# Two-layer retention and gated-linear-attention backbone: norms and slab splits taken off GpSimd

## Chip, cores, metric

One NeuronCore of a Trainium2 chip runs the whole program. The metric is device microseconds of one execution, the median of several runs. Before the change three runs took 1653.16, 1654.71 and 1655.32 us.

## What is computed

Two layers act on a stream of 512 latent tokens and a prefix of 256 context tokens, 1024 features each, in float32:

```python
for layer in range(DEPTH):                       # DEPTH = 2
    need_ctx = layer < DEPTH - 1
    sh1, sc1, g1, sh2, sc2, g2 = split(silu(c) @ ada_w[layer] + ada_b[layer])
    hx = modulate(rmsnorm(x, norm1_g[layer]), sh1, sc1)
    hc = modulate(rmsnorm(ctx, norm1_g[layer]), csh1, csc1)
    mx, mc = hybrid_mixer(hx, hc, ...)           # 4 retention heads, 4 GLA heads
    x = x + g1 * (mx @ w_out[layer])
    hx = modulate(rmsnorm(x, norm2_g[layer]), sh2, sc2)
    x = x + g2 * squared_relu_mlp(hx, w_mlp1[layer], w_mlp2[layer])
    if need_ctx:
        ...
return rmsnorm(x, final_g)
```

`modulate(h, shift, scale)` is `h * (1 + scale) + shift`. The mixer projects the normed tokens with `w_in` (3616 columns) into queries, keys, values, gates and the low-rank decay, runs both scans of each head over chunks, and normalises each head before the output projection. Layer 2 needs no context output.

## The kernel before

**Layout.** The activations stand transposed: eight tiles `x_0` to `x_7` of 128 features by 768 tokens, latents in columns 0 to 511 and context in 512 to 767. Every float32 product is made of three products of rounded parts, `hi*hi + hi*lo + lo*hi` (`mm3`, lines 433 to 436; `project`, lines 438 to 457). So each weight slab of 128x1024 and each activation is split into a rounded `hi` and a rest `lo`.

**Slabs.** A `Slab` is loaded by SP into one of four `raw` buffers; `split` (lines 241 to 245) writes `hi` with ScalarE (ACT) and `lo` with the slab's `engine`, VectorE (DVE) by default, GpSimd (POOL) for a few. Slabs 5 and 6 of layer 2's `w_in` go to GpSimd (lines 691, 692). `hi` and `lo` have six buffers each. `run` (lines 386 to 424) walks a plan of items; before an item it splits the slabs that the item needs and `item.ahead` more (4 unless the item says otherwise), and after an item with slabs up to four more than it needed.

**Norms.** `Norm.stat` (line 485) sums squares over features with a matmul by `ones_d` (tile `st_n`), and ACT makes the reciprocal root from it (tile `ssum_n`, lines 494 and 495). `Norm.apply` (lines 506 to 523) then turns each of the eight tiles into `hi` and `lo`. It has two forms. The usual one: DVE writes `xn = x*scale*rstd` (L519), ACT writes `hi` (L521), DVE writes `lo` (L523). The other one, for every third tile (`kk % 3 == 2`, tiles 2 and 5): GpSimd writes `x*rstd` (L512), ACT writes `hi` (L514) and the scaled value again (L515), DVE writes `lo` (L517). A chain runner (`Chains`) keeps three tiles under way and interleaves their steps with other work, one step at each tick.

**Layer 2's start.** While TensorE (PE) still works on the last MLP products of layer 1 for the context columns (tiles `pm`, whose sums DVE adds to `x` on L537), the norm of the latents runs. Then the item `firsts0` (function `together`) multiplies tile after tile with the first three slabs 0, 1 and 3 into three banks `ps_d`, `ps_gq`, `ps_gk`; after tile 5 it calls the norm of the context columns. `firsts1` does slabs 0 and 3 for the context, then the item `firsts` evacuates those banks, and the values `vg` follow with slabs 5 to 8 (block `vg0`, tiles `ps_vg`).

**Evacuating heads.** `dup_evac` (lines 720 to 735) copies a bank that holds two heads, 64 rows each, into one 128-row tile per head, the 64 rows twice (`d` is the half of the destination, `i` the head). In layer 1, for heads 0 and 1, half `d = 0` goes to ACT and half `d = 1` to DVE. All else is ACT's.

**Order.** In-layer stages stand in the table `SCHEDULE` (lines 107 to 132); each row's entries are run in order, in both layers. `g2qk` is the stage in which DVE multiplies the queries (L847) and keys (L848) of GLA head 2, the third head, by their decays; `g2S` makes their score products (tiles `psf`, `psb`, L869). `qa0` and `qb0` project the retention queries of heads 0 and 1 (`ps_qa`, `ps_qb`); DVE evacuates `ps_qa` with L950 and L951. `g0A` and its like make the decay (tile `pgl`, L814). `g1N` makes a head's norm (tile `hs`, L794).

PSUM has seven banks in rotation (`ps`): a new tile waits until the tile seven allocations back has been read.

Of the kernel before, what the change touches and what calls it, by code (L numbers as in the profile page):

```python
# [12 lines left out]
AF = mybir.ActivationFunctionType  # L13
ALU = mybir.AluOpType
# [100 lines left out]
vr2 g0D g1K tabs  # L115
gq1 g1D g0O g3A
gk1 g1O g0N g3B
qa0 g2qk g1N g3C
qb0 g2S g2K g3qk
ka0 g3S g3K g2D  # L120
kb0 g3D g2O
# [17 lines left out]
def build(ctx: ExitStack, tc, a):  # L139
    nc = tc.nc  # L140
# [14 lines left out]
    ch = Chains()  # L155

    def bank(name):
        return ps.tile([P, 512], F32, tag="ps", name=name)

    def work(name, dt=F32):  # L160
        return mp.tile([P, T], dt, tag="m", name=name)

    def temp(name):
        return tmp_pool.tile([P, LAT], F32, tag="t", name=name)

    def f32(ap):
        return ap.bitcast(F32)
# [275 lines left out]
    def project(pt, slab, c0, acts, t0, t1, ks=None, first=0, last=None):  # L443

        ks = range(len(acts)) if ks is None else ks
        last = len(acts) - 1 if last is None else last
        out = pt[:, 0 : t1 - t0]
        for k in ks:
            acts[k].ready(ch, t0, t1)
            xh, xl = acts[k].hi[:, t0:t1], acts[k].lo[:, t0:t1]  # L450
            w = slice(c0 + k * P, c0 + k * P + P)
            if isinstance(slab, RankSlab):
                nc.tensor.matmul(out, slab.hi[:, w], xh, start=k == first, stop=False)
                nc.tensor.matmul(out, slab.hi[:, w], xl, start=False, stop=k == last)
            else:
                mm3(out, slab.hi[:, w], slab.lo[:, w], xh, xl, k == first, k == last)
        ch.tick()


    class Norm:  # L460
# [42 lines left out]
                    op0=ALU.add, op1=ALU.mult,  # L503
                )

        def apply(self, kk, l, shift, v, t0, t1, pool=False):
            hh, hl = self.out[kk].hi[:, t0:t1], self.out[kk].lo[:, t0:t1]
            xn = temp(f"xn_{self.name}_{kk}_{t0}")[:, 0 : t1 - t0]
            x, rstd = xs[kk][:, t0:t1], self.ssum[:, t0:t1]
            scale, bias = self.s[:, v, kk : kk + 1], mod[l][:, v, shift + kk : shift + kk + 1]  # L510
            if pool:
                nc.gpsimd.tensor_mul(xn, x, rstd)  # L512
                yield
                nc.scalar.activation(hh, xn, AF.Identity, scale=scale, bias=bias)  # L514
                nc.scalar.activation(xn, xn, AF.Identity, scale=scale, bias=bias)  # L515
                yield
                nc.vector.tensor_sub(hl, xn, f32(hh))  # L517
            else:
                nc.vector.scalar_tensor_tensor(xn, x, scale, rstd, op0=ALU.mult, op1=ALU.mult)  # L519
                yield  # L520
                nc.scalar.activation(hh, xn, AF.Identity, bias=bias)  # L521
                yield
                nc.vector.scalar_tensor_tensor(hl, xn, bias, f32(hh), op0=ALU.add, op1=ALU.subtract)  # L523

        def apply_all(self, l, shift, v, t0, t1, ks=range(KK)):

            for kk in ks:
                if self.out[kk] is None:
                    self.out[kk] = Act(
                        work(f"hh_{self.name}_{kk}", F32R), work(f"hl_{self.name}_{kk}", F32R)  # L530
                    )
            for kk in ks:
                c = ch.queue(self.apply(kk, l, shift, v, t0, t1, kk % 3 == 2))
                self.out[kk].made.append((t0, t1, c))

    def residual(kk, pt, l, gate, v, t0, t1):
# [34 lines left out]
    def start_project(q, groups):  # L571
        for j in START:
            for t0, t1 in groups:
                if q == 0:
                    acc0[j, t0] = bank(f"ps0_{j}_{t0}")
                project(acc0[j, t0], sl0[j], 0, norm0.out, t0, t1, (2 * q, 2 * q + 1), 0, KK - 1)
# [23 lines left out]
    def quarter_step(q):  # L600
        quarter_chain[q] = quarter(q)
        start_project(q - 1, ALLG)

    def quarter_finish(q):
        quarter_end(q, quarter_chain[q])
        quarter_norm(q, ALLG)
        for _ in range(6):
            ch.tick()
# [3 lines left out]
    def load_late():  # L612
        for name, shape in (("delta", [P, P]), ("ramp", [P, 2, P]), ("cosT", [P, LAT]), ("sinT", [P, LAT])):
            late[name] = load_const(name, shape)
# [42 lines left out]
    def layer(l, norm):  # L657
# [8 lines left out]
        pre = f"L{l}."  # L666
        tabs = {}

        def start():
            raw = temp(f"upraw_{l}")  # L670
            nc.sync.dma_start(raw, a["upw"][l])
            upw = tabs["upw"] = tp.tile([P, NH, P], F32R, tag="upw", name=f"upw_{l}")
            raw = raw.rearrange("p (h m) -> p h m", h=NH)
            nc.scalar.copy(upw, raw)
            nc.vector.tensor_sub(upw[96:128], raw[96:128], f32(upw[96:128]))

            tabs["ret"] = tp.tile([P, NH, 3, P], F32, tag="rtab", name=f"rtab_{l}")
# [10 lines left out]
            nc.vector.tensor_scalar(rtab[:, h, 1:3], rtab[:, h, 1:3], RET_SCALE, None, op0=ALU.mult)  # L688

        sl = [(Slab if j else RankSlab)(w_in[j], f"wi{l}_{j}") for j in range(29)]  # L690
        for j in (5, 6) if l else ():
            sl[j].engine = nc.gpsimd

        def feat(j, name, groups, evac):
            def fn():
# [26 lines left out]
        def dup_evac(lst, hp2, nm, sc):  # L722
            def ev(p_, t0, t1):
                for i in range(2):
                    h = 2 * hp2 + i
                    if t0 == 0:
                        lst[h] = work(f"{nm}_{l}_{h}")
                    for d in range(2):
                        dst, src = lst[h][64 * d : 64 * d + 64, t0:t1], p_[64 * i : 64 * i + 64]
                        if d and l == 0 and hp2 == 0:  # L730
                            nc.vector.tensor_scalar(dst, src, sc, None, op0=ALU.mult)
                        else:
                            nc.scalar.mul(dst, src, sc)

            return ev
# [358 lines left out]
        if l == 0:  # L1094

            def head():
                start()
                load_late()
                for j, _, groups, ev in firsts:
                    for t0, t1 in groups:  # L1100
                        ev(acc0[j, t0][:, 0 : t1 - t0], t0, t1)

            plan = [
                Item(pre + "norm", start_norms, ahead=0),
                Item(pre + "q3", lambda: quarter_step(3), ahead=0),
                Item(pre + "q3n", lambda: quarter_finish(3), ahead=0),
                Item(pre + "q3p", lambda: start_project(3, ALLG), ahead=0),
                Item(pre + "head", head, ahead=4),
            ]
        else:  # L1110
            done = []

            def together(i):

                todo = [(j, bank(f"ps_{nm}_1_{groups[i][0]}"), *groups[i], ev)
                        for j, nm, groups, ev in firsts if i < len(groups)]
                for kk in range(KK):
                    for j, pt, t0, t1, _ in todo:
                        project(pt, sl[j], 0, act, t0, t1, [kk], 0, KK - 1)
                    if kk == 5 and i == 0:  # L1120
                        next_norm(norm, l, 1)
                done.extend(todo)

            def evacuate():
                while done:
                    _, pt, t0, t1, ev = done.pop(0)
                    ev(pt[:, 0 : t1 - t0], t0, t1)

            plan = [
                Item(pre + "start", start),  # L1130
                Item(pre + "firsts0", lambda: together(0), [sl[j] for j in (0, 1, 3)]),
                Item(pre + "firsts1", lambda: together(1), [sl[j] for j in (0, 3)]),
                Item(pre + "firsts", evacuate),
            ]
# [214 lines left out]
    for l in range(DEPTH):  # L1349
        items, norm = layer(l, norm)  # L1350
        plan += items
# [97 lines left out]
```

## Time and profile before

| | before |
|---|---|
| runs | 1653.16, 1654.71, 1655.32 us (median 1654.71) |
| the profiled execution | 1652.87 us, of which its span 1651.1 us |
| mean granted TensorE clock | 0.998 |
| PE busy | 1619.0 us, 98% of the span, 9306 matmuls |
| DVE, ACT, POOL busy | 945.2 us (57%), 629.5 us (38%), 191.2 us (12%) |
| DMA | 173.82 MB, mean 105 GB/s |

A matmul's busy time reaches past the start of the next, so a gap in PE is shorter than the time between the starts suggests. The times of a row are counted from the span's start. "x2" at the end of a row means two instructions merged, with the time of both; what stands in brackets is the idle time of the engine before it and what ended it.

### The profile page before, as it was taken

The page shows a single profiled execution, that of the slowest core. Times are in us where ns is not written, and L with a number is a line of the kernel's source. Part 1 is how long each engine was busy: PE and PEld are TensorE (multiplying, and loading weights), DVE is VectorE, ACT ScalarE, POOL GpSimd, SP SyncE. Part 2 cuts the span into 40 slices and gives each one's busy share as a digit, 9 for nine tenths or more (in the row PEclk, how much of TensorE's full clock was granted, in tenths as well). Part 3 has the DMA queues.
Part 4 walks back from the last instruction along what each step waited for, and adds up shares of the span by engine and source line. Part 5 has one row for each costly group of instructions (what it writes and reads, how often), then busy time and mean ns, then how long its engine had stood idle before and what let it go on. Part 6 is the DMA issues. An engine that isn't in the chain of part 4 may idle for free. (4 is left out here: it accounts for less than half of the span.)

```text
span 1651.1 us, 23033 instructions
## 1 busy us (share of the span) xinstructions
PE 1619.0 (98%) x9306; PEld 1386.0 (84%) x9306; DVE 945.2 (57%) x1494; ACT 629.5 (38%) x1085; POOL 191.2 (12%) x211
## 2 busy tenths in 40 slices
PE   6999999999999999999999999999999999999997
PEld 4778788888898888888888888888889988888887
DVE  5675664554755555555556476688466743343445
ACT  5635333562532222222212246363464623223232
POOL 2000022110111010110101121002111301010010
PEclk9999999999999999999999999999999999999999
DMA  9443333122323333333433222121124322323311
GB/s 327 147 142 129 127 115 116 39 101 78 103 90 128 115 128 112 118 102 115 128 115 128 90 81 79 52 76 52 52 67 139 116 92 99 100 92 102 102 64 52
DMA packets 57611, 173.82 MB, mean 105 GB/s; under 512 B 6208, under 2 KB 17792, under 8 KB 57504
## 3 DMA queue, kind: packets, MB, share of 16 engines
q1 hardware_dynamic: 55232, 164.85, 30.5%
q0 software_dynamic: 2272, 7.50, 1.3%
q8 instruction: 73, 1.20, 0.3%
q14 instruction: 34, 0.28, 0.1%
HBM read 168.13 MB, written 4.19 MB: 104 GB/s over the span
## 5 line engine op out<-in xcount | busy, mean ns | idle before, releaser
L440 PE MATMUL pm<-yl,hi_m 128*128 128x512 f32 (+1 forms) x808 | 279.7, 346 | 1.1 <-DVE yl L517 0.6
L439 PE MATMUL pm<-yh,hi_m 128*128 128x512 f32 (+1 forms) x808 | 279.8, 346 | 0.0
L439 PE MATMUL pm<-hidh,hi_m 128*128 128x512 f32 (+1 forms) x800 | 279.1, 349 | 0.0
L441 PE MATMUL pm<-yh,lo_m 128*128 128x512 f32 (+1 forms) x808 | 278.7, 345 | 0.0
L440 PE MATMUL pm<-hidl,hi_m 128*128 128x512 f32 (+1 forms) x800 | 278.4, 348 | 0.0
L441 PE MATMUL pm<-hidh,lo_m 128*128 128x512 f32 (+1 forms) x800 | 277.2, 347 | 0.0
L1220 ACT ACTIVATE relu<-pm 128x512 f32<-128x512 f32 (+1 forms) x101 | 51.3, 508 | 493.0 <-PE pm L441 493.0
L1224 DVE TENSOR_TENSOR hidl<-relu,hidh 128x512 fp32r<-128x512 f32 (+1 forms) x101 | 61.7, 613 | 290.0 <-POOL relu L1222 290.0
L537 DVE SCALAR_TENSOR_TENSOR x<-pm,mod,x 128x512 f32<-128x512 f32 (+1 forms) x200 | 117.6, 640 | 108.8 <-PE pm L441 108.8
L1222 POOL TENSOR_TENSOR relu<-relu 128x512 f32<-128x512 f32 (+1 forms) x101 | 90.6, 898 | 755.9 <-ACT hidh L1221 755.6
L440 PEld LDWEIGHTS pm<-yl,hi_m 128*128 128x128 f32 x808 | 153.1, 189 | 20.8 <-DVE yl L523 1.2
L439 PEld LDWEIGHTS pm<-yh,hi_m 128*128 128x128 f32 x808 | 153.0, 189 | 19.9 <-issue 1.2
L439 PEld LDWEIGHTS pm<-hidh,hi_m 128*128 128x128 f32 x800 | 151.4, 189 | 21.2 <-issue 1.1
L441 PEld LDWEIGHTS pm<-yh,lo_m 128*128 128x128 f32 x808 | 153.0, 189 | 18.7
L441 PEld LDWEIGHTS pm<-hidh,lo_m 128*128 128x128 f32 x800 | 151.1, 189 | 19.6
L440 PEld LDWEIGHTS pm<-hidl,hi_m 128*128 128x128 f32 x800 | 151.4, 189 | 19.0 <-issue 0.2
L245 DVE TENSOR_TENSOR lo_m<-raw_m,hi_m 128x1024 fp32r<-128x1024 f32 x126 | 153.9, 1222 | 10.1 <-ACT hi_m L244 10.1
L244 ACT CAST hi_m<-raw_m 128x1024 fp32r<-128x1024 f32 x128 | 129.8, 1040 | 52.1 <-DMA raw_m<-in_w_mlp 28.8
L345 DVE SCALAR_TENSOR_TENSOR adaacc<-adaw,cs,adaacc 128x1024 f32<-128x1024 f32 x84 | 103.9, 1278 | 0.0
L245 DVE TENSOR_TENSOR lo_wi<-raw_wi,hi_wi 128x1024 fp32r<-128x1024 f32 x54 | 66.4, 1247 | 28.1 <-ACT hi_wi L244 27.9
L439 PE MATMUL pwo<-yh,hi_wo 128*128 128x256 f32 (+1 forms) x224 | 70.9, 316 | 0.1
L440 PE MATMUL pwo<-yl,hi_wo 128*128 128x256 f32 (+1 forms) x224 | 70.3, 314 | 0.3 <-DVE yl L1068 0.3
(306 smaller groups left out, 2934.2 us busy)
## 6 DMA issues: line engine op xcount, KB each, us to landing
raw_m<-in_w_mlp SPq DMA_DIRECT2D x128, 512.0 KB, 3.5
adaw<-in_ada_w SPq DMA_DIRECT2D x80, 512.0 KB, 3.8
raw_wi<-in_w_in SPq DMA_DIRECT2D x58, 512.0 KB, 4.4
adaw<-in_ada_w SPq DMA_DIRECT2D x32, 256.0 KB, 6.0
raw_wo<-in_w_out SPq DMA_DIRECT2D x16, 512.0 KB, 3.5
x<-in_xT POOLq DMA_DIRECT2D x8, 384.0 KB, 8.0
x<-in_xT SPq DMA_DIRECT2D x8, 256.0 KB, 5.0
raw_wob<-in_w_out SPq DMA_DIRECT2D x4, 512.0 KB, 3.9
```

Of the source, the lines that this page charges most:

```text
L244: nc.scalar.copy(self.hi, self.raw)
L245: self.engine.tensor_sub(self.lo, self.raw, f32(self.hi))
L345: nc.vector.scalar_tensor_tensor(acc[:, v], w, c, acc[:, v], op0=ALU.mult, op1=ALU.add)
L439: nc.tensor.matmul(out, wh, xh, start=first, stop=False)
L440: nc.tensor.matmul(out, wh, xl, start=False, stop=False)
L441: nc.tensor.matmul(out, wl, xh, start=False, stop=last)
L537: nc.vector.scalar_tensor_tensor(xs[kk][:, t0:t1], pt[:, 0 : t1 - t0], mod[l][:, v, gate + kk : gate + kk + 1], xs[kk][:, t0:t1], op0=ALU. ...
L1220: nc.scalar.activation(r, pt[:, 0 : t1 - t0], AF.Relu)
L1222: nc.gpsimd.tensor_mul(r, r, r)
L1224: nc.vector.tensor_sub(a_.lo[:, t0:t1], r, f32(a_.hi[:, t0:t1]))
```

## The change

1. `Norm.apply` loses its GpSimd form. Tiles 2 and 5 of every norm take the usual form: for each of the norms' column groups (16 tile pieces in all) a GpSimd product (L512) and an ACT pass (L515) go, a DVE product (L519) comes.
2. Slabs 5 and 6 of layer 2's `w_in` get their `lo` from DVE.
3. Layer 2's items `start` and `firsts0` get `ahead=0`: no slabs beyond those needed are split before them.
4. In layer 1 the bank of heads 0 and 1 is evacuated with head 0's tile by ACT alone and head 1's by DVE alone.
5. `g2qk` moves ahead of `qa0` in the table.

```diff
-qa0 g2qk g1N g3C
+g2qk qa0 g1N g3C
...
-        def apply(self, kk, l, shift, v, t0, t1, pool=False):
+        def apply(self, kk, l, shift, v, t0, t1):
...
-            if pool:
-                nc.gpsimd.tensor_mul(xn, x, rstd)
-                yield
-                nc.scalar.activation(hh, xn, AF.Identity, scale=scale, bias=bias)
-                nc.scalar.activation(xn, xn, AF.Identity, scale=scale, bias=bias)
-                yield
-                nc.vector.tensor_sub(hl, xn, f32(hh))
-            else:
-                nc.vector.scalar_tensor_tensor(xn, x, scale, rstd, op0=ALU.mult, op1=ALU.mult)
-                yield
-                nc.scalar.activation(hh, xn, AF.Identity, bias=bias)
-                yield
-                nc.vector.scalar_tensor_tensor(hl, xn, bias, f32(hh), op0=ALU.add, op1=ALU.subtract)
+            nc.vector.scalar_tensor_tensor(xn, x, scale, rstd, op0=ALU.mult, op1=ALU.mult)
+            yield
+            nc.scalar.activation(hh, xn, AF.Identity, bias=bias)
+            yield
+            nc.vector.scalar_tensor_tensor(hl, xn, bias, f32(hh), op0=ALU.add, op1=ALU.subtract)
...
-                c = ch.queue(self.apply(kk, l, shift, v, t0, t1, kk % 3 == 2))
+                c = ch.queue(self.apply(kk, l, shift, v, t0, t1))
...
-        for j in (5, 6) if l else ():
-            sl[j].engine = nc.gpsimd
...
-                        if d and l == 0 and hp2 == 0:
+                        if i and l == 0 and hp2 == 0:
                             nc.vector.tensor_scalar(dst, src, sc, None, op0=ALU.mult)
                         else:
                             nc.scalar.mul(dst, src, sc)
...
-                Item(pre + "start", start),
-                Item(pre + "firsts0", lambda: together(0), [sl[j] for j in (0, 1, 3)]),
+                Item(pre + "start", start, ahead=0),
+                Item(pre + "firsts0", lambda: together(0), [sl[j] for j in (0, 1, 3)], ahead=0),
```

What this does to the order of instructions, at three places. First, DVE at the norm of the latents ahead of layer 2; `xn_n_1_K` and `hl_n_1_K` are tile K's product and rest, `x_2` the sum over the last MLP product. Before:

```order
L523 SCALAR_TENSOR_TENSOR hl_n_1_1_8394<-xn_n_1_1_0_8421,mod_150,hh_n_1_1_8393 128x512
L519 SCALAR_TENSOR_TENSOR xn_n_1_3_0_8442<-x_3_3369,mods_n_1_8384,ssum_n_1_8224 128x512
L517 TENSOR_TENSOR hl_n_1_2_8396<-xn_n_1_2_0_8434,hh_n_1_2_8395 128x512
L519 SCALAR_TENSOR_TENSOR xn_n_1_4_0_8449<-x_4_3371,mods_n_1_8384,ssum_n_1_8224 128x512
L537 SCALAR_TENSOR_TENSOR x_2_3367<-pm_0_7_2_512_8409,mod_149,x_2_3367 128x256
...
L523 SCALAR_TENSOR_TENSOR hl_n_1_3_8398<-xn_n_1_3_0_8442,mod_150,hh_n_1_3_8397 128x512
L523 SCALAR_TENSOR_TENSOR hl_n_1_4_8400<-xn_n_1_4_0_8449,mod_150,hh_n_1_4_8399 128x512
```

After:

```order
L511 SCALAR_TENSOR_TENSOR xn_n_1_2_0_8426<-x_2_3363,mods_n_1_8376,ssum_n_1_8216 128x512
L515 SCALAR_TENSOR_TENSOR hl_n_1_1_8386<-xn_n_1_1_0_8413,mod_150,hh_n_1_1_8385 128x512
L511 SCALAR_TENSOR_TENSOR xn_n_1_3_0_8433<-x_3_3365,mods_n_1_8376,ssum_n_1_8216 128x512
L515 SCALAR_TENSOR_TENSOR hl_n_1_2_8388<-xn_n_1_2_0_8426,mod_150,hh_n_1_2_8387 128x512
L511 SCALAR_TENSOR_TENSOR xn_n_1_4_0_8440<-x_4_3367,mods_n_1_8376,ssum_n_1_8216 128x512
L529 SCALAR_TENSOR_TENSOR x_2_3363<-pm_0_7_2_512_8401,mod_149,x_2_3363 128x256
...
L515 SCALAR_TENSOR_TENSOR hl_n_1_3_8390<-xn_n_1_3_0_8433,mod_150,hh_n_1_3_8389 128x512
L511 SCALAR_TENSOR_TENSOR xn_n_1_5_0_8452<-x_5_3369,mods_n_1_8376,ssum_n_1_8216 128x512
L245 TENSOR_TENSOR lo_wi_5_8457<-raw_wi_5_8370,hi_wi_5_8456 128x1024
L515 SCALAR_TENSOR_TENSOR hl_n_1_4_8392<-xn_n_1_4_0_8440,mod_150,hh_n_1_4_8391 128x512
```

DVE has two products of tiles 2 and 5 and one slab split more; the sum `x_2` has one more product ahead of it.

Second, ACT at the norm of the context columns in layer 2 (`hi_wi_J` are slabs, `hh_n` the norm's `hi` tiles). Before:

```order
L674 CAST upw_8551<-upraw_8549 128x512
L244 CAST hi_wi_6_8557<-raw_wi_6_8463 128x1024
L244 CAST hi_wi_7_8563<-raw_wi_7_8555 128x1024
L494 ACTIVATE ssum_n_1_8224<-st_n_1_512_8618,epst 128x256
L495 ACTIVATE ssum_n_1_8224<-ssum_n_1_8224 128x256
...
L521 ACTIVATE hh_n_1_7_8405<-xn_n_1_7_512_8651,mod_150 128x256
L244 CAST hi_wi_8_8716<-raw_wi_8_8561 128x1024
```

After:

```order
L666 CAST upw_8541<-upraw_8539 128x512
L494 ACTIVATE ssum_n_1_8216<-st_n_1_512_8596,epst 128x256
L495 ACTIVATE ssum_n_1_8216<-ssum_n_1_8216 128x256
...
L513 ACTIVATE hh_n_1_7_8397<-xn_n_1_7_512_8627,mod_150 128x256
L244 CAST hi_wi_6_8650<-raw_wi_6_8454 128x1024
L244 CAST hi_wi_7_8656<-raw_wi_7_8648 128x1024
L244 CAST hi_wi_8_8704<-raw_wi_8_8654 128x1024
```

Slabs 6 and 7 now stand behind the norm of the context instead of ahead of its root; on DVE the split of slab 7, which stood ahead of the first product of this norm, and that of slab 6 stand behind its last rest in the same way.

Third, DVE around `g2qk` in layer 2. Before:

```order
L833 TENSOR_TENSOR gt_3_9417<-gt_3_9417,gst_3_9513 128x768
L245 TENSOR_TENSOR lo_wi_17_9522<-raw_wi_17_9429,hi_wi_17_9521 128x1024
L950 TENSOR_TENSOR rq_0_0_9550<-ps_qa_0_0_9525,c_cosT 64x512
L951 TENSOR_TENSOR rq_0_0_9550<-ps_qa_0_0_9525,c_sinT 64x512
L950 TENSOR_TENSOR rq_0_1_9551<-ps_qa_0_0_9525,c_cosT 64x512
L951 TENSOR_TENSOR rq_0_1_9551<-ps_qa_0_0_9525,c_sinT 64x512
L847 TENSOR_TENSOR gq_2_9377<-gq_2_9377,gt_2_8827 128x512
L848 TENSOR_TENSOR gk_2_9460<-gk_2_9460,gl_2_8828 128x768
```

After:

```order
L823 TENSOR_TENSOR gt_3_9405<-gt_3_9405,gst_3_9501 128x768
L837 TENSOR_TENSOR gq_2_9365<-gq_2_9365,gt_2_8815 128x512
L838 TENSOR_TENSOR gk_2_9448<-gk_2_9448,gl_2_8816 128x768
L245 TENSOR_TENSOR lo_wi_17_9512<-raw_wi_17_9417,hi_wi_17_9511 128x1024
L940 TENSOR_TENSOR rq_0_0_9540<-ps_qa_0_0_9515,c_cosT 64x512
L941 TENSOR_TENSOR rq_0_0_9540<-ps_qa_0_0_9515,c_sinT 64x512
```

The two products stand ahead of a slab split and of the four operations that evacuate `ps_qa`. On PE the order is the same except for one place in layer 1, where the two `hs` products of `g1N` come ahead of the transposes `adat` (L268) instead of behind them. SP's queue keeps its order. POOL has 18 instructions less.

## Rows read from the trace of the kernel before

**Rows 1.** Waits of PE: who for whom, us in total, times, the longest.

```profile
PE st_n L492 <- DVE ssum_n L475: 1.8, 2, 1.3
PE adat L268 <- ACT adarow L263: 1.7, 3, 0.7
PE ps_d L453 <- ACT hh_n L521: 1.5, 1, 1.5
...
PE psf L869 <- DVE gk L848: 1.0, 1, 1.0
PE ps_gq L439 <- DVE x L537: 1.0, 1, 1.0
PE pm L440 <- DVE yl L517: 0.6, 2, 0.4
```

**Rows 2.** Timeline of PE, layer 1: start, length, engine, line, tiles, [idle before].

```profile
70.95 0.38 PE L814 MATMUL pgl<-dT,upw 128*128 128x256 f32 x1 [1.43 <-ACT vg L775]
71.63 0.50 PE L439 MATMUL ps_vg<-hi_wi,hh_n 128*128 128x512 f32 x1 [0.30 <-ACT vg L775]
```

**Rows 3.** Timeline of ACT, the first evacuations of layer 1.

```profile
60.59 0.59 ACT L733 ACTIVATE gq<-ps 64x512 f32<-64x512 f32 x1
...
67.84 0.38 ACT L733 ACTIVATE gk<-ps 64x256 f32<-64x256 f32 x1 [0.80 <-DVE gk L731]
...
70.13 1.45 ACT L775 COPY vg<-ps_vg 128x128 f32<-128x128 f32 x8
```

**Rows 4.** Timeline of ACT, the first evacuations of layer 2.

```profile
1003.70 2.40 ACT L733 ACTIVATE gq<-ps_gq 64x512 f32<-64x512 f32 x4
...
1008.81 1.55 ACT L733 ACTIVATE gk<-ps_gk 64x256 f32<-64x256 f32 x4
...
1012.42 0.78 ACT L775 COPY vg<-ps_vg 128x128 f32<-128x128 f32 x4
```

**Rows 5.** Timeline of DVE around `g2qk` in layer 2.

```profile
1103.93 1.22 DVE L245 TENSOR_TENSOR lo_wi<-raw_wi,hi_wi 128x1024 fp32r<-128x1024 f32 x1
...
1108.48 0.95 DVE L848 TENSOR_TENSOR gk<-gk,gl 128x768 f32<-128x768 f32 x1
```

**Rows 6.** Timeline of DVE, the norms ahead of layer 2.

```profile
971.10 2.45 DVE L519 SCALAR_TENSOR_TENSOR xn_n<-x,mods_n,ssum_n 128x512 f32<-128x512 f32 x2
...
975.90 1.56 DVE L517 TENSOR_TENSOR hl_n<-xn_n,hh_n 128x512 fp32r<-128x512 f32 x1
...
981.21 2.90 DVE L519 SCALAR_TENSOR_TENSOR xn_n<-x,mods_n,ssum_n 128x512 f32<-128x512 f32 x1
...
992.48 2.58 DVE L245 TENSOR_TENSOR lo_wi<-raw_wi,hi_wi 128x1024 fp32r<-128x1024 f32 x1 [1.18 <-ACT hi_wi L244]
994.98 1.80 DVE L519 SCALAR_TENSOR_TENSOR xn_n<-x,mods_n,ssum_n 128x256 f32<-128x256 f32 x2
```

**Rows 7.** Timeline of POOL in the same stretch.

```profile
981.00 2.56 POOL L245 TENSOR_TENSOR lo_wi<-raw_wi,hi_wi 128x1024 fp32r<-128x1024 f32 x1 [4.08 <-ACT hi_wi L244]
```

**Rows 8.** Timeline of DVE, the same operations while POOL is idle.

```profile
48.24 1.42 DVE L519 SCALAR_TENSOR_TENSOR xn_n<-x,mods_n,ssum_n 128x512 f32<-128x512 f32 x2
...
1275.21 0.47 DVE L519 SCALAR_TENSOR_TENSOR xn_n<-x,mods_n,ssum_n 128x256 f32<-128x256 f32 x1
1275.60 0.47 DVE L537 SCALAR_TENSOR_TENSOR x<-pwo,mod,x 128x256 f32<-128x256 f32 x1
```

**Rows 9.** Timeline of PE: the sum of the context norm of layer 2.

```profile
990.63 0.70 PE L492 MATMUL st_n<-ssum_n,ones_d 128*128 128x256 f32 x2 [1.33 <-DVE ssum_n L475]
```

**Rows 10.** Timeline of ACT: the root for the context norm of layer 2.

```profile
992.35 0.47 ACT L494 ACTIVATE ssum_n<-st_n,epst 128x256 f32<-128x256 f32 x1
```

**Rows 11.** Timeline of PE where `vg0` of layer 2 begins.

```profile
1003.65 0.40 PE L439 MATMUL ps_vg<-hi_wi,hh_n 128*128 128x512 f32 x1
```

**Rows 12.** PE in two windows: length, busy (instructions), granted clock, DMA share, GB/s.

```profile
997.90:1001.40 3.50, 3.50 (x18) 0.53 0.14 59
1001.40:1004.00 2.60, 2.60 (x22) 0.98 0.00 0
```

## Prediction

> **What bounds the kernel now.** I read the busy times first (the table above). PE is busy 98% of the span, so time can come only from the few places where PE stands still. The second view is the list of waits: whom PE waits for. Of the waits that bear on this change, a reader should see how short they are and that each names one engine [rows 1]: 1.5 us for ACT's `hi` of the context norm in layer 2, 1.3 us for the sum of squares ahead of it, 1.0 us for DVE's evacuation of the old MLP bank, 1.0 us for the keys of `g2qk`, 0.7 us for an ACT copy ahead of `adat`, 0.6 us for rests of layer 2's second norm. In layer 1, PE stands 1.43 and 0.30 us because ACT copies `vg` too late [rows 2]. The third view is the timeline around these places. It gives the causes, and one more loss: after the waits in layer 2's start, 18 matmuls take 3.50 us at a granted clock of 0.53 (the 1.2 GHz level), where 22 of the same size then take 2.60 us at 0.98 [rows 12]. At that pace 18 need 2.1 us, so 1.4 us are lost though PE counts as busy.
>
> **First evacuation, layer 1.** ACT and DVE write halves of the same tile, and they alternate: ACT's eight copies run from 60.59 to 68.22 us, each waiting for DVE's half [rows 3]. In layer 2 ACT makes such copies alone without a wait, at 0.60 us (four in 2.40) and 0.39 us (four in 1.55) [rows 4]. With a head per engine ACT needs 4 x 0.60 + 4 x 0.39 = 4.0 us instead of 7.6 and is through at 64.6, 3.6 us earlier. The copies of `vg` then begin at 66.5 instead of 70.13, and the first bank is free by 67.3; PE asks for it at 70.95 - 1.43 = 69.5. The second bank's product ends only just before that, and its four copies take 0.7 us (half of 1.45), so it is free at about 69.5 too. Both waits go: 1.7 us. Bounds 0.8 (the second copies slip) and 2.0.
>
> **`g2qk` moved.** Its keys end at 1108.48 + 0.95 = 1109.4; PE waited 1.0 us for them. What now stands behind them is a slab split of 1.22 us and four evacuations that fill the time until the two products begin [rows 5], so they end some 3.9 us earlier, near 1105.5. The wait goes: 1.0 us. The price is that `ps_qa` is evacuated 1.6 us later (the two products); its bank is next wanted after one projection and the score products, about a microsecond behind that. Bounds 0.2 and 1.0. In layer 1 the same move brings the `hs` products ahead of `adat`, into the 0.7 us in which PE waits for ACT's copy [rows 1]; their input was made before. 0.7 us, bounds 0 and 0.7.
>
> **Norm without GpSimd, layer 2's start.** This is the largest term.
> Ahead of layer 2 DVE has no idle time until the sum of squares is through, so its work there sets when PE may go on. With POOL idle, a product of 512 columns takes 0.71 us (two in 1.42), and operations of 256 columns follow each other every 0.39 us [rows 8]. Beside POOL's norm and slab work they take far longer [rows 6]: two products 2.45 us, one rest 1.56 us, one product 2.90 us, which ends half a microsecond after POOL's 2.56 us split [rows 7]. The excess is 1.03 + 0.85 + 2.19 = 4.1 us. Added are two products (2 x 0.71) and the split of slab 5 (1.22, as in [rows 5]): 2.6 us. The sum comes 1.4 us earlier, at 989.2. The evacuation for which PE waits 1.0 us at the start has +0.71 and -1.9 us ahead of it, so that wait goes, and PE, arriving 1.0 us earlier at the sum, still waits some 0.9 us there instead of 1.33 [rows 9].
> ACT's root could have begun at 990.63 + 0.70 = 991.3; it began at 992.35, behind slabs 6 and 7 [rows 10]. And DVE began the first product only at 994.98, behind slab 7's split of 2.58 us [rows 6]. Both stand behind the norm now: root at 989.9, first product at 990.9, 4.1 us earlier. Sixteen operations at 0.40 us and the first handover of 0.7 us end at 998.0. PE reaches the context columns near 993.5 and needs 40 x 0.118 = 4.7 us at full pace [rows 12], so it ends near 998.5; now `vg0` begins at 1003.65 [rows 11]. That is 5.1 us, of which the slow stretch is 1.4.
> What it costs: slabs 6, 7 and 8 are split after the norm. ACT's casts come from 997.2 on, DVE's splits end near 999.4, 1000.6 and 1001.8 at 1.22 us each. PE wants slab 6 about 1.6 us into `vg0`, at 1000.1, and another every 1.4 us. The margin is about half a microsecond. ACT's evacuations move up by only 3.1 us, so its copies of `vg` begin at 1009.3 instead of 1012.42 [rows 4], and PE waits about 0.3 us for the second bank. Net 4.8 us; bounds 1.0 (first rival) and 5.6.
> The Trainium skill speaks against this part: Perfetto Trace Analysis, section Optimizing Scalar/DVE Operations, says that offloading work to other engines, even GPSIMD, may make sense if DVE is saturated, which it is here (though it adds that between those two it might not help). By that rule, taking the work back would lengthen the stretch; by the rows it shortens it. The rule's outcome is the third rival below.
>
> **The other norms.** The second norm of layer 2 gains the waits for its rests, 0.6 us [rows 1], for the same reason; bounds -0.9 (two more products of 0.47 us [rows 8], nothing relieved) and 0.9. In the first norm of layer 1 and its second norm PE hardly waits for rests, so the two products more are hidden behind PE's work and paid for by POOL's silence: 0, bounds -0.5 and 0.5. ACT loses a pass per piece, which nobody waits for.
>
> **Sum.** 1.7 + 1.0 + 0.7 + 4.8 + 0.6 = 8.8 us. On the profiled execution of 1652.87 us that gives 1644.1. The median of the runs, 1654.71, is 1.8 us above that execution, so the forecast for the median is **1645.9 us**.
>
> **Rivals.**
> First, *the start of layer 2 stays held by what now follows the norm*. If a pair of product and rest costs 1.1 us instead of 0.8, the rests end 2.4 us later, slab 6 comes after PE wants it, and a pause there costs a slow stretch of 1.4 us again. The term falls to 1.0, the sum to 5.0: 1649.7. For it speaks the margin of half a microsecond; against it that the rests' pace is taken from rows.
> Second, *the waits only move to the next in line*. If ACT's evacuations keep their time in layer 2 (copies of `vg` at 1012.42), PE gets its bank 3.1 us later than walked and the term is 1.7; if in layer 1 DVE's half holds the bank and `ps_qa`'s bank is late, those give 0.8 and 0.2. With the 0.7 that is 3.4 or less: 1651.3 and above, within what a measurement of this kernel can tell from no change (0.2%, 3.3 us). Against it: ACT's string has nothing else ahead of it.
> Third, slower: *DVE is saturated and not relieved*. If its long operations ahead of layer 2 are not POOL's doing, the sum comes 2.6 us later instead of 1.4 earlier, the root at 994.9, and 16 operations at 0.90 us (half of 1.80 [rows 6]) end near 1010.0. `vg0` begins 6.4 us later than now, and the second norm loses 0.9. With 1.7, 1.0 and 0.7 gained that is 3.9 us slower: 1658.6. It decides once `vg0` begins later than about 1006.1, when the loss at both norms outweighs the 3.4 us. Against it: with POOL idle the same operations take 0.71 and 0.39 us.
>
> **Numbers.** Forecast 0.72, first rival 0.15, second 0.08, third 0.05. Faster by over 0.2%: forecast and first rival, 0.87; within 0.2%: 0.08; slower: 0.05. All upper bounds together are 10.7 us, 1644.0; the three runs differ by 2.2 us, so the range begins 1.5 us below that, at 1642.5. It goes to 1650.5, which takes in the first rival with half that scatter and leaves out the other two.
>
> **What would show it.** Right: no idle bracket at the sixth `pgl` in layer 1; ACT's eight copies there without gaps, done by 65 us; DVE's 512-column products ahead of layer 2 all near 0.74 us; `vg0` of layer 2 beginning about 5 us earlier relative to the last MLP product than now, with no window at half clock before it; no wait of `psf` for the keys. A wait of about 0.9 us for the sum of squares remains. Wrong: PE waiting for `lo` of slabs 6 to 8 in `vg0`, or products of DVE above 1 us with POOL idle.

## Result and profile after

The changed kernel took 1643.48 us (median of four runs, 1642.86 to 1644.87) beside 1654.43 us of the kernel before on the same chip: a ratio of 0.9936, 95% interval 0.9918 to 0.9953. Run again with other kernels (`c_after` below) it gave 1643.13 us beside 1654.48, ratio 0.9933 (0.9919 to 0.9947). The forecast was 1645.9 us, the range 1642.5 to 1650.5.

The busy times of the page, after the change:

```profile
PE 1616.7 (98%) x9306; PEld 1385.6 (84%) x9306; DVE 942.0 (57%) x1512; ACT 619.3 (38%) x1069; POOL 167.0 (10%) x193
```

POOL lost 24 us of work and ACT 10. DVE, which took over the products and two slab splits, is busy 3 us *less* than before. The waits of PE after (who for whom, us in total, times, the longest):

```profile
PE st_n L492 <- DVE ssum_n L475: 1.5, 2, 1.0
PE adat L268 <- ACT adarow L263: 0.9, 2, 0.5
PE pm L440 <- DVE yl L515: 0.7, 4, 0.2
...
PE ps_vg L439 <- ACT vg L765: 0.2, 1, 0.2
```

Of [rows 1], the waits for `hh_n`, for the keys and for `x` ahead of `ps_gq` are gone, that for `adat` is halved, and the 1.43 us at `pgl` [rows 2] are gone. The wait for the sum is 1.0 instead of 1.3. For the rests of layer 2's second norm (`yl`) PE waits almost as before: 0.7 us in four pieces, against 0.9 in four (0.6 in [rows 1] and this row of the kernel before):

```profile
PE pm L440 <- DVE yl L523: 0.3, 2, 0.2
```

**Layer 1's first evacuation**, the timeline of ACT and then PE (start, length, engine, line, tiles):

```profile
62.46 1.99 ACT L723 ACTIVATE gq<-ps 64x512 f32<-64x512 f32 x4
64.47 1.99 ACT L723 ACTIVATE gk<-ps 64x512 f32<-64x512 f32 x4
66.48 2.00 ACT L244 CAST hi_wi<-raw_wi 128x1024 fp32r<-128x1024 f32 x2
68.39 0.76 ACT L765 COPY vg<-ps_vg 128x128 f32<-128x128 f32 x4
...
71.48 0.47 PE L439 MATMUL ps_vg<-hi_wi,hh_n 128*128 128x512 f32 x1
```

ACT's eight copies take 4.0 us without a gap, against 7.6 in [rows 3], and the bracket of PE is gone.

**Layer 2's start**, DVE:

```profile
969.32 1.42 DVE L511 SCALAR_TENSOR_TENSOR xn_n<-x,mods_n,ssum_n 128x512 f32<-128x512 f32 x2
...
978.01 1.22 DVE L245 TENSOR_TENSOR lo_wi<-raw_wi,hi_wi 128x1024 fp32r<-128x1024 f32 x1
...
988.96 0.88 DVE L511 SCALAR_TENSOR_TENSOR xn_n<-x,mods_n,ssum_n 128x256 f32<-128x256 f32 x2 [1.03 <-ACT ssum_n L495]
...
996.37 3.50 DVE L245 TENSOR_TENSOR lo_wi<-raw_wi,hi_wi 128x1024 fp32r<-128x1024 f32 x3 [0.45 <-ACT hi_wi L244]
```

The pair of products that took 2.45 us beside POOL [rows 6] takes 1.42. Slab 5's split is the row of 1.22 us; slabs 6 to 8 follow the norm in 3.50 us. PE, in the same stretch:

```profile
987.26 0.70 PE L492 MATMUL st_n<-ssum_n,ones_d 128*128 128x256 f32 x2 [1.00 <-DVE ssum_n L475]
...
996.55 0.40 PE L439 MATMUL ps_vg<-hi_wi,hh_n 128*128 128x512 f32 x1
...
1008.85 0.50 PE L439 MATMUL ps_vg<-hi_wi,hh_n 128*128 128x512 f32 x1 [0.18 <-ACT vg L765]
```

From the sum to `vg0` it is 9.3 us now; it was 13.0 (1003.65 less 990.63, [rows 9, 11]).

**A loss that was not forecast** stands ahead of all this: the first profile of the changed kernel is 2 us *behind* that of the kernel before at 40 us. PE in two windows (length, busy (instructions), granted clock, DMA share, GB/s), first profile:

```profile
30.00:34.50 4.50, 2.52 (x17) 1.00 1.09 356
34.50:39.00 4.50, 4.47 (x38) 0.62 1.09 349
```

and `c_after`, the same program:

```profile
30.00:34.50 4.50, 3.18 (x25) 1.00 1.10 357
34.50:39.00 4.50, 4.48 (x49) 1.00 1.09 349
```

### The profile page after: what moved, and what is told of

It is laid out like the page before. It is cut to its first block, busy times and chain, and to the rows that moved or that the text cites. A ratio compares the mean times of both kernels' runs of the same rounds, so it can differ in the third digit from the quotient of the medians.

```text
span 1643.1 us, 23030 instructions
## 1 busy us (share of the span) xinstructions
PE 1616.7 (98%) x9306; PEld 1385.6 (84%) x9306; DVE 942.0 (57%) x1512; ACT 619.3 (38%) x1069; POOL 167.0 (10%) x193
```

## Where the time went, place by place

All kernels here issue 9306 matmuls, in the same order but for one place in layer 1. So one can take the start of the same matmul in two profiles and follow the difference (the lag): it stays constant, mostly to 0.05 us, and jumps at a few places. The table has these jumps against `c_after` (plus: the kernel loses time there). "Start" is what has gathered by 40 us.

| kernel | start | first norm, layer 1 | evacuation, layer 1 | `hs`/`adat` | second norm, layer 1 | layer 2's start | `g2qk` | second norm, layer 2 | ratio to before (95%) |
|---|---|---|---|---|---|---|---|---|---|
| before | -0.80 | 0.38 | 2.59 | 0.76 | 0.43 | 4.94 | 1.02 | 0.23 | 1 |
| changed, first profile | 1.59 | -0.01 | 0 | 0 | 0 | 0 | -0.06 | 0.01 | 0.9936 (0.9918 to 0.9953) |
| c_after | 0 | 0 | 0 | 0 | 0 | 0 | 0 | 0 | 0.9933 (0.9919 to 0.9947) |
| e1_norm_pool | 1.39 | -0.06 | 0 | 0 | 0.71 | 1.50 | 0.03 | 0.23 | 0.9956 (0.9944 to 0.9969) |
| e2_pool_slabs | -0.60 | 0.07 | 0 | 0 | 0 | 1.93 | 0.01 | -0.27 | 0.9946 (0.9932 to 0.996) |
| e3_split_ahead | -0.90 | -0.02 | 0 | 0 | 0 | 1.02 | 0.03 | -0.27 | 0.9943 (0.993 to 0.9955) |
| e4_halves | 0.71 | -0.01 | 2.49 | 0 | 0 | 0.03 | 0.01 | -0.29 | 0.9953 (0.994 to 0.9965) |
| e5_table | -0.70 | 0 | -0.01 | 0.76 | 0 | -0.04 | 1.05 | 0.01 | 0.9946 (0.9934 to 0.9959) |
| e6_dve_slabs | 0.14 | 0 | 0 | 0 | 0 | -0.05 | -0.02 | -0.84 | 0.9932 (0.992 to 0.9945) |
| e7_idle_pool | -0.41 | -0.01 | 0 | 0 | 0 | 1.39 | -0.02 | -0.27 | 0.9944 (0.993 to 0.9957) |
| b1_ahead_only | -0.65 | 0.40 | 2.39 | 0.76 | 0.40 | 2.56 | 1.00 | 0.23 | 0.9986 (0.9977 to 0.9995) |
| e8_slab5_late | 0.30 | 0 | 0 | 0 | 0 | -0.18 | -0.02 | 0.02 | 0.9932 (0.9919 to 0.9945) |
| e9_both | 0 | -0.01 | 0 | 0 | 0 | -0.20 | -0.01 | -0.83 | 0.9933 (0.9919 to 0.9947) |
| e10_relu | 3.16 | 0.01 | 0 | 0 | 0 | -0.21 | -0.03 | -1.33 | 0.9928 (0.9915 to 0.9941) |

Against the kernel before, the jumps add up to 10.35 us, less 0.80 at the start: 9.6 us, the difference of the two spans (1651.1 and 1641.5). The medians differ by 11.35; the profiled execution of before (1652.87) is 1.6 us below the median of its runs beside `c_after`, which is all but 0.2 us of the rest. The last columns of kernels that are alike there say how far to trust the table: 0.05 us at most places, 0.3 us at layer 2's second norm (the kernels with the norms and splits of the changed kernel there stand at about 0 or at about -0.27), and the start not at all (-0.90 to 3.16). The three profiles with the old form of the norms all show 0.23 at that place.

## Experiments

My theory: DVE's operations are held up while POOL works beside them, and the slabs split ahead of the context norm delayed it; each part pays at its own place. Rivals: DVE is saturated and POOL relieves it; waits only move on; and, for the unforeseen loss at 34 us, that the change causes it.

### Work on POOL that nobody needs (e7_idle_pool)

```diff
+    scr = const.tile([P, P], F32, name="scr")
...
             nc.vector.scalar_tensor_tensor(xn, x, scale, rstd, op0=ALU.mult, op1=ALU.mult)
+            if self.name == "n1_1" and t0 == 0 and kk in (2, 5):
+                for c0 in range(t0, t1, P):
+                    nc.gpsimd.tensor_mul(scr, xs[kk][:, c0 : c0 + P], self.ssum[:, c0 : c0 + P])
```

> The changed kernel with eight products on GpSimd added in the first half of layer 1's last norm (four of 128 columns each at pieces 2 and 5), written to a tile that nobody reads: the work of DVE, ACT and PE is unchanged and nobody waits for POOL. My theory: DVE's 512-column operations that lie beside them take 1.2 us or more instead of 0.75, the sum of squares ahead of layer 2 comes 1 to 2.5 us later, PE waits longer at the sum or at the evacuation ahead of ps_gq by that much: 0.7 to 2.5 us above the changed kernel. Rival (DVE's operations there were long for another reason, such as a transfer or ACT's traffic): DVE's durations and the time unchanged, within 0.3 us at the landmarks.

DVE and then POOL, and PE ahead of `ps_gq`:

```profile
967.33 1.76 DVE L513 SCALAR_TENSOR_TENSOR xn_n<-x,mods_n,ssum_n 128x512 f32<-128x512 f32 x2
969.01 0.94 DVE L520 SCALAR_TENSOR_TENSOR hl_n<-xn_n,mod,hh_n 128x512 fp32r<-128x512 f32 x1
...
976.04 0.75 DVE L520 SCALAR_TENSOR_TENSOR hl_n<-xn_n,mod,hh_n 128x512 fp32r<-128x512 f32 x1
...
967.21 6.53 POOL L516 TENSOR_TENSOR scr<-x,ssum_n 128x128 f32<-128x128 f32 x8 [4.60 <-ACT ssum_n L497]
...
974.74 0.50 PE L439 MATMUL ps_gq<-hh_n,hi_wi 128*128 128x512 f32 x1 [0.92 <-DVE x L534]
```

While POOL's eight small products run, until 973.7, each DVE operation takes 0.94 us; behind them the same operation takes 0.75. Nothing waits for POOL, and the place loses 1.39 us. So DVE is slowed by the mere fact that POOL works beside it. My size for one operation (1.2 us or more) was too high for POOL work in such small pieces, the sum was in range.

### One part at a time taken back

**The norm's GpSimd form (e1_norm_pool).**

```diff
-                c = ch.queue(self.apply(kk, l, shift, v, t0, t1))
+                c = ch.queue(self.apply(kk, l, shift, v, t0, t1, kk % 3 == 2))
```

with `apply` as it was.

> The changed kernel with the GpSimd form of the norms back (pieces 2 and 5 of each norm: product on POOL, two passes on ACT); all else as changed. My theory (DVE is slowed while POOL works beside it): in the last norm of layer 1, ahead of layer 2, one or two of DVE's 512-column products beside POOL's take 1.2 us or more instead of 0.75, the excess eats the two products saved, and PE's wait for the sum of squares stays within 0.6 us of the changed kernel's 1.0; in the context norm the three handovers and POOL's two products bring the last piece 0.3 to 1.5 us later. Time 0.5 to 3 us above the changed kernel. Rival (DVE is saturated and GpSimd relieves it): the sum comes 1.4 us earlier, the second norm of layer 2 loses waits, 1 to 2 us below the changed kernel. A second question is the 2.05 us that the changed kernel lost between 30 and 39 us, in layer 1's start, against the kernel before: if the norm's form caused it, matmuls there run at full clock here and the loss is gone; if it is a late transfer, it comes and goes whatever the kernel.

POOL, DVE and PE:

```profile
969.72 1.29 POOL L512 TENSOR_TENSOR xn_n<-x,ssum_n 128x512 f32<-128x512 f32 x1 [4.65 <-ACT ssum_n L495]
...
969.78 2.45 DVE L519 SCALAR_TENSOR_TENSOR xn_n<-x,mods_n,ssum_n 128x512 f32<-128x512 f32 x2
...
977.25 0.50 PE L439 MATMUL ps_gq<-hh_n,hi_wi 128*128 128x512 f32 x1 [0.98 <-DVE x L537]
```

One product of 1.29 us on POOL adds 1.03 us to two on DVE (2.45 against 1.42); saving a product and losing that is no gain. The evacuation for which `ps_gq` waits comes late again, and layer 2's start loses 1.50 us. It also loses 0.71 us at layer 1's second norm, where I had put nothing. The slow stretch at 34 us is here too, with the old form.

**Slabs 5 and 6 on GpSimd (e2_pool_slabs).**

```diff
+        for j in (5, 6) if l else ():
+            sl[j].engine = nc.gpsimd
```

> The changed kernel with the splits of slabs 5 and 6 of layer 2 back on GpSimd; all else as changed. My theory: a split on POOL takes 2.4 us or more and slows DVE's operations beside it, the products of layer 1's last norm from 0.75 to 1.2 us or more; the sum of squares comes 0.5 to 1.5 us later than in the changed kernel although DVE has a split of 1.2 us less. Slab 6 on POOL now comes behind the context norm and vg0 waits for it or not by under 1 us. Time 0.5 to 2.5 us above the changed kernel. Rival (relief): the sum comes 1.2 us earlier, the wait of 1.0 us ahead of the sum goes, 1 us below the changed kernel.

POOL, DVE, and PE at the sum:

```profile
975.76 2.47 POOL L245 TENSOR_TENSOR lo_wi<-raw_wi,hi_wi 128x1024 fp32r<-128x1024 f32 x1 [13.25 <-ACT hi_wi L244]
...
975.90 2.88 DVE L515 SCALAR_TENSOR_TENSOR hl_n<-xn_n,mod,hh_n 128x512 fp32r<-128x512 f32 x1
...
986.15 0.70 PE L492 MATMUL st_n<-ssum_n,ones_d 128*128 128x256 f32 x2 [2.01 <-DVE ssum_n L475]
```

PE in a window behind the sum (length, busy, granted clock, DMA share, GB/s):

```profile
988.50:991.00 2.50, 2.50 (x7) 0.55 0.02 7
```

A rest that takes 0.75 us elsewhere begins 0.14 us after POOL's split and ends 0.55 us after that split is done: 2.1 of its 2.88 us are more than it needs elsewhere. DVE has 1.22 us of split less to do and is a microsecond later all the same. PE waits 2.01 us for the sum, and after that wait the granted clock falls to the lower level (0.55 in the window, 7 matmuls in 2.5 us): a microsecond late became 1.93. The Trainium skill, SBUF — State Buffer, section Who interferes with whom, says that a DVE instruction with two SBUF inputs contends with a GpSimd instruction that reads SBUF, and that the order of issue decides which of the two blocks. By that rule this rest, which began second, blocks until POOL's split is done, and the trace agrees (it ends at 978.78, the split at 978.23).

**Slabs split ahead of the norm (e3_split_ahead).**

```diff
-                Item(pre + "start", start, ahead=0),
-                Item(pre + "firsts0", lambda: together(0), [sl[j] for j in (0, 1, 3)], ahead=0),
+                Item(pre + "start", start),
+                Item(pre + "firsts0", lambda: together(0), [sl[j] for j in (0, 1, 3)]),
```

> The changed kernel with slabs 6 and 7 split ahead of layer 2's norm again (the two ahead=0 taken back); all splits on DVE and ACT, none on POOL. My theory: two splits of 1.22 us and two casts of 0.98 us stand again between the root and the first product of the context norm; the root begins 0.5 to 1.1 us late and the first product 2.0 to 2.8 us late, the matmuls on the context columns fall to the half clock for some microseconds again, and vg0 begins 3 to 4 us later than in the changed kernel. Of this the second bank's wait of 0.2 to 0.3 us comes back. Time 2.5 to 4 us above the changed kernel. Rival (the gain there came from POOL's silence alone): vg0 begins within 1 us of the changed kernel, time within 1 us.

ACT, then DVE:

```profile
984.53 2.00 ACT L244 CAST hi_wi<-raw_wi 128x1024 fp32r<-128x1024 f32 x2
...
985.61 2.36 DVE L245 TENSOR_TENSOR lo_wi<-raw_wi,hi_wi 128x1024 fp32r<-128x1024 f32 x2 [0.17 <-ACT hi_wi L244]
987.88 0.87 DVE L511 SCALAR_TENSOR_TENSOR xn_n<-x,mods_n,ssum_n 128x256 f32<-128x256 f32 x2
```

A miss: 1.02 us, not 2.5 to 4. The first product comes 3.1 us after the sum's matmul instead of 1.7, so the norm is 1.4 us later. But the last piece is then only just late: PE's waits are short, no stretch at the low clock follows, and 0.4 us return at the bank of `vg`. Both splits take 2.36 us together here; in the kernel before, one of them alone took 2.58 [rows 6], beside this split on POOL:

```profile
991.57 2.40 POOL L245 TENSOR_TENSOR lo_wi<-raw_wi,hi_wi 128x1024 fp32r<-128x1024 f32 x1 [8.02 <-ACT hi_wi L244]
```

**The order alone, on the kernel before (b1_ahead_only).** The same two lines changed in the kernel before, nothing else.

> The kernel before with one part of the change alone: no slab split ahead of layer 2's first norm (the two ahead=0); slab 6 is then split by POOL behind the norm. In the changed kernel, taking this part back cost only about 1.0 us in layer 2's start, where I had expected 2.5 to 4. Theory now (the order costs more while POOL works, because a split on POOL stretches DVE's next split to 2.6 us): alone on the kernel before it gives 2 to 3.5 us in layer 2's start, among it the half-clock stretch. Rival (the parts are worth the same alone as together): 1.0 us below the kernel before.

Layer 2's start takes 2.56 us more than in `c_after` where the kernel before takes 4.94: the order alone gives 2.4 us, in the expected range, and the stretch at half clock is gone. What is left shows at the next place, where `vg0` waits for slab 6, which POOL now splits behind the norm:

```profile
1002.69 0.50 PE L440 MATMUL ps_vg<-lo_wi,hh_n 128*128 128x512 f32 x1 [0.56 <-POOL lo_wi L245]
```

So the order is worth 2.4 us while POOL works and 1.0 once it doesn't. The three parts taken back alone cost 1.50, 1.93 and 1.02: 4.45 of the 4.94 us. The 0.5 left over is what they cost only together.

**The halves (e4_halves).**

```diff
-                        if i and l == 0 and hp2 == 0:
+                        if d and l == 0 and hp2 == 0:
```

> The changed kernel with the old evacuation of layer 1's first tiles (ACT and DVE write halves of one tile); all else as changed. My theory: ACT's eight copies wait for DVE's halves again and take 7 to 8 us instead of 4, PE stands 1.4 us ahead of a bank of the sixth product and 0.3 us ahead of vg's, together 1.7 to 2.2 us, and nothing downstream gives it back: 1.7 to 2.2 us above the changed kernel. Rival (the halves were no cause, the waits went because PE arrived 2 us later after its slow stretch at 34 us): the waits stay below 0.5 us, time within 0.5 us.

ACT, then PE:

```profile
63.50 1.00 ACT L723 ACTIVATE gq<-ps 64x512 f32<-64x512 f32 x2 [1.29 <-DVE gq L721]
...
71.97 0.38 PE L804 MATMUL pgl<-dT,upw 128*128 128x256 f32 x1 [1.33 <-ACT vg L765]
72.65 0.50 PE L439 MATMUL ps_vg<-hi_wi,hh_n 128*128 128x512 f32 x1 [0.30 <-ACT vg L765]
```

ACT's gaps for DVE's halves and PE's two waits are back, although this profile also has the late start. By the lag the two cost 2.1 us, more than their brackets (1.63), and two small steps of 0.2 follow, at 75 us and where `ps_vr` begins. 2.49 us in all, above the expected 2.2.

**The table's row (e5_table).**

```diff
-g2qk qa0 g1N g3C
+qa0 g2qk g1N g3C
```

> The changed kernel with the row of the table as before (qa0 ahead of g2qk); all else as changed. My theory: psf of head 2 waits for DVE's evacuation of the keys again in layer 2 (about 1.0 us), and adat waits for ACT's copy in layer 1 (0.7 us): the first matmuls behind those two places begin 1.06 and 0.7 us later against the changed kernel, nothing else moves, 1.5 to 1.9 us above the changed kernel. Rival (the waits only moved to ps_qa's bank or the score products): under 0.5 us.

PE in layer 2:

```profile
1101.32 0.34 PE L859 MATMUL psf<-gq,gk 64*128 64x128 f32 x1 [1.03 <-DVE gk L838]
```

1.05 us there and 0.76 at `adat`, as expected, and nothing elsewhere.

### Going further in the same direction

**All slab splits on DVE (e6_dve_slabs).**

```diff
-        if l:
-            wo2[0].engine = nc.gpsimd
...
-        if l:
-            for j in (1, 3):
-                m1[j].engine = nc.gpsimd
```

> The changed kernel with the last three slab splits that are on GpSimd (one of the output projection's second set and two of the first MLP weights, all in layer 2) moved to DVE as well. My theory: beside POOL's two MLP splits of 2.4 to 2.5 us DVE's operations take 1.6 to 2.6 us instead of 0.47 to 0.95, so DVE gains more than the two splits of 1.22 us cost it; PE's waits for rests in layer 2's second norm (five of about 0.17 us) shrink, 0.3 to 1.0 us below the changed kernel. Rival (DVE is full there and GpSimd relieves it): the rests come 1 to 2 us later and the time is 0.5 to 2 us above.

In the changed kernel, DVE and POOL ahead of the rests for which PE waits:

```profile
1274.21 2.62 DVE L511 SCALAR_TENSOR_TENSOR xn_n<-x,mods_n,ssum_n 128x256 f32<-128x256 f32 x1
...
1284.34 2.31 DVE L475 TENSOR_TENSOR ssum_n<-ssum_n,sq_n 128x256 f32<-128x256 f32 x1 [0.54 <-ACT sq_n L473]
...
1274.06 2.49 POOL L245 TENSOR_TENSOR lo_m<-raw_m,hi_m 128x1024 fp32r<-128x1024 f32 x1 [11.77 <-ACT hi_m L244]
...
1283.95 2.41 POOL L245 TENSOR_TENSOR lo_m<-raw_m,hi_m 128x1024 fp32r<-128x1024 f32 x1 [7.40 <-ACT hi_m L244]
```

and PE's wait in e6_dve_slabs:

```profile
PE pm L440 <- DVE yl L515: 0.3, 2, 0.2
```

A product of 0.48 us took 2.62 and a sum of 0.42 took 2.31, each beside a split on POOL. With the splits on DVE the waits fall from 0.7 to 0.3 and 0.84 us are gained at this place (the kernels that are alike there scatter by 0.3). The three splits moved together, so what each is worth is not shown. The median, 0.9932 of before, is not to be told from the changed kernel's.

**Slab 5 behind the norm as well (e8_slab5_late).** The planner runs 3 slabs ahead instead of 4 in the last MLP products of layer 1 (their items get `few(last)` too).

```diff
-                advance(i + 1, need + AHEAD)
+                advance(i + 1, need + it.after)
...
+        def few(last):
+            return {"ahead": 3, "after": 3} if last and l == 0 else {}
...
-                    plan.append(Item("nx0", lambda: next_norm(nxt, l + 1, 0)))
+                    plan.append(Item("nx0", lambda: next_norm(nxt, l + 1, 0), **few(True)))
```

> The changed kernel with one slab split fewer ahead of the norm: in layer 1's last MLP products the planner runs 3 slabs ahead instead of 4, so slab 5 of layer 2 (1.22 us on DVE, 1.0 us on ACT) stands behind the context norm too, with 6, 7 and 8. Theory: DVE has no idle time ahead of the sum of squares, so the sum comes 1.1 us earlier and PE's wait of 1.0 us for it goes; the norm ends 1.0 us earlier; slab 5's split ends about 996.5 on the first profile's clock, ahead of vg0 (997.6 by then), and 6, 7 and 8 by 1.2 us each against 1.4 us per slab in vg0. 0.7 to 1.1 us below the changed kernel. Rival (four splits behind the norm are one too many): vg0 waits for slab 5 or 6, and the time is the changed kernel's or up to 2 us above.

PE at the sum and in `vg0`, and DVE:

```profile
984.86 0.70 PE L493 MATMUL st_n<-ssum_n,ones_d 128*128 128x256 f32 x2
...
995.25 0.51 PE L441 MATMUL ps_vg<-lo_wi,hh_n 128*128 128x512 f32 x1 [0.70 <-DVE lo_wi L246]
...
993.97 4.63 DVE L246 TENSOR_TENSOR lo_wi<-raw_wi,hi_wi 128x1024 fp32r<-128x1024 f32 x4 [0.45 <-ACT hi_wi L245]
```

Half a miss. The wait for the sum is gone and PE is 1.1 us earlier; then `vg0` waits 0.70 us for slab 5, whose split ends at 995.2, and 0.3 us is lost as the matmuls get under way. 0.18 us remain: the rival was right that four splits behind the norm are one too many.

**Both together (e9_both), and the relu squares on DVE (e10_relu).**

```diff
-            nc.gpsimd.tensor_mul(r, r, r)
+            nc.vector.tensor_mul(r, r, r)
```

> Slab 5 late and all slab splits on DVE together. Theory: the two places lie 300 us apart and add up: 1.0 us at layer 2's start and 0.5 to 0.9 us at its second norm, 1.2 to 1.9 us below the changed kernel, the best of all versions. Rival: as one of the two alone.

> The version before (slab 5 late, all splits on DVE) with the MLP's squares of relu on DVE instead of GpSimd, 0.7 us each. Theory (POOL's work costs only where DVE is what is waited for): in the MLP DVE is not waited for but at the second norm, where the squares add their 0.7 us each to a full DVE; the rests of layer 2's second norm come later, 0 to 2 us above the version before. Rival (any work on POOL beside DVE costs more than it saves): 0.3 to 1 us below it.

e9_both keeps both steps (-0.20 and -0.83), 1.05 us in its profile, below the 1.2 expected as slab 5 gave little. In its median, 1643.07 us, that isn't seen. In e10_relu my theory missed and the rival held: although DVE has more to do, layer 2's second norm gains another 0.5 us (-1.33), with PE's wait for the rests down to one:

```profile
PE pm L441 <- DVE yl L516: 0.2, 1, 0.2
```

Its median, 1641.20 us, is the lowest of all (ratio 0.9928, 0.9915 to 0.9941; the changed kernel beside it 0.9933, 0.9919 to 0.9947), but the intervals overlap and its five runs spread from 1640.6 to 1645.0. Its profile lost 3.16 us at the start.

**The loss at the start (c_after).** The changed kernel, unchanged.

> The changed kernel once more, beside the next three on one chip. What is open: in its first profile it lost 2.1 us between 30 and 39 us of layer 1's start, where the granted clock fell to 0.58; of the seven profiles since, two show such a stretch (with the norms' new form and with the old one) and five do not. Theory (a late transfer or the clock itself, not the change): there or not, and every landmark behind it stands to the first profile as a constant, within 0.4 us, up to the second norm of layer 2. Median 1642 to 1644.5 us. Rival (the change brings the loss on): the stretch is there again and the profile within 0.5 us of the first.

The stretch isn't there, and the first profile's lag is 1.59 at 40 us and 1.56 at the end. The rival fell: one program has the loss in one execution and not in the next. Of the fourteen profiles four have it (the first of the changed kernel, e1_norm_pool, e4_halves, e10_relu). Whether the change makes it likelier can't be told: the two kernels with the old norms and the old slabs were profiled once each.

## Why the prediction was right, and where it was off

The forecast was 8.8 us by its steps; the profiles give 10.35 less 0.80 at the start. The mechanism held at the places that carry most of the sum. That the time came out only 2.4 us below the forecast (1643.48 against 1645.9) owes something to luck: 0.4 us that did not come at layer 2's second norm was outweighed by 0.8 at two norms put at nothing and 0.9 at the first evacuation. Point by point, against the row of the kernel before in the table:

- **First evacuation, 1.7 us:** 2.59, above its upper bound of 2.0 (2.49 when taken back alone). Mechanism right, term too small: it counted the two brackets, and the lag shows half a microsecond more there as PE restarts and 0.4 behind it. ACT's copies did take 4.0 us.
- **`g2qk` and `hs`:** 1.0 and 0.7 forecast, 1.02 and 0.76 measured, no price seen for `ps_qa`.
- **Layer 2's start, 4.8 us:** 4.94. The walk held in its parts: the sum comes 1.6 us earlier (forecast 1.4), PE waits 1.0 for it (0.9), `vg0` begins 5.3 earlier (5.1, clock included), and the second bank takes back 0.4 (0.3). One step was too simple: of the 4.1 us by which the first product was to come earlier, 1.4 were the sum's, and it put the other 2.7 down to slabs 6 and 7 standing ahead. Both parts came (1.6 and 2.65), but with POOL idle the two splits ahead delay the first product by only 1.4 (e3_split_ahead), and the order taken back alone costs 1.02; with POOL at work it is worth 2.4. Slab 6's split on POOL had made slab 7's on DVE twice as long (2.58 us against 2.36 for two).
- **First rival:** the margin of half a microsecond for slab 6 was real. In the first profile of the changed kernel the first of the three splits behind the norm ends at 997.6, and PE wants it 1.6 us into `vg0`, at 998.15. With one split more behind the norm (e8_slab5_late) `vg0` waits 0.70, and with slab 6 on POOL in the kernel before (b1_ahead_only) 0.56. In e2_pool_slabs, where POOL splits slab 6 too, it doesn't wait: PE comes later there, after its stretch at the low clock.
- **Second rival, waits that move on:** only the 0.4 us at the second bank.
- **Third rival, DVE saturated:** DVE had no idle time ahead of the sum, but part of its busy time was standing still for POOL. e1_norm_pool, e2_pool_slabs and e7_idle_pool each lose where this rival gains or stands still. The advice of the Trainium skill in Perfetto Trace Analysis, section Optimizing Scalar/DVE Operations, holds here by its second half only, that offloading between these two might not help.
- **Second norm of layer 2, 0.6 us:** failed. 0.23 measured. PE's waits for the rests were to go and fell only from 0.9 to 0.7. The step put POOL's presence down to the norm's products; the splits of `m1` stayed on POOL, and with them (and one of the output projection) moved to DVE the waits fall to 0.3 (e6_dve_slabs).
- **Other norms, 0:** layer 1's first norm gained 0.38 and its second 0.43, together above the bound of 0.5. e1_norm_pool, with the old form, shows 0.71 at the second, so the form of the norms is what counts there; it shows nothing at the first, which it reached 2 us later than the kernel before. Why the first gained is not shown.
- **From profile to median:** the sum was set off from the profiled execution and 1.8 us were added back for the median. That held: 11.35 us between medians is 9.6 and 1.6 and what scatter leaves.

## What to carry over

Read "this engine is saturated" together with how long the same operation takes elsewhere: where DVE's operations are several times as long beside POOL as without it, POOL's help is the load. Compare profiles of kernels with the same matmul order by the lag of each matmul; half a microsecond then has a place, where medians scatter by more. Work moved behind a wait is free only up to a count (three splits here; four were forecast to fit and did not), and a wait on PE that grows by 1.0 us can cost 1.9 when the clock falls behind it.

## What the runs showed of the hardware that I had not expected

- How long a DVE operation is held up goes with the length of POOL's operation beside it. Beside one split of 2.47 us a DVE operation of 0.75 us took 2.88; beside products of 128 columns (eight in 6.53 us) each DVE operation took 0.94.
- Programs that are the same up to there differ by up to 4 us in their first 40 us (-0.90 to 3.16), and one program run twice by 1.6. In the four profiles that are late, the granted clock falls to between 0.50 and 0.64 from about 34.5 us. In two of them PE had just waited 0.8 and 0.9 us for a transfer. In e1_norm_pool it had been as busy (3.18 of 4.50 us) as in `c_after`, where the clock stayed up; what decides it stays open.
